# A convolution module's input product: six of sixteen channel blocks take both halves of the activations in one product and add two partial sums

## The chip, the cores and the metric

One core of a Trainium2 chip runs the whole program. The metric is the device time of one execution in microseconds (us); smaller is better. The kernel before was timed three times; the profile is a further execution, recorded by the hardware profiler.

## What is computed

The reference is a small decoder trunk on one sequence of 256 tokens with 2048 channels, all in float32. It has two mixer layers, each followed by a dense MLP, and a last RMSNorm. The change lies in the first mixer, a causal convolution module:

```python
def conv_module(h, w_in, b_in, dw, dw_b, ln_g, ln_b, w_out, b_out):
    u = h @ w_in + b_in                       # (256 x 2048) @ (2048 x 4096)
    a, gate = jnp.split(u, 2, axis=-1)
    v = a * jax.nn.sigmoid(gate)
    v = lax.conv_general_dilated(v, dw[:, None, :], window_strides=(1,),
        padding=[(CONV_WIDTH - 1, 0)], ...)   # 31 taps along the tokens, each channel alone
    v = layer_norm(v + dw_b, ln_g, ln_b)
    return jax.nn.silu(v) @ w_out + b_out

for i in range(DEPTH):                        # DEPTH = 2
    x = x + mixer_i(rms_norm(x, mix_norm[i])) # i = 0: conv_module, i = 1: an S5 layer
    x = x + mlp(rms_norm(x, mlp_norm[i]), w_up[i], w_down[i])
return rms_norm(x, final_norm)
```

## The kernel before

**Products in float32r.** TensorE (PE) multiplies in the type float32r. To keep the accuracy, each float32 operand is split into a high part `hi`, rounded to float32r, and a remainder `lo`. A product is then the sum of three: weight hi by activation hi, weight hi by activation lo, and weight lo by activation hi. Weights stream from memory by the DMA queue of SyncE (`fetch`, L92) into three buffers `raw`; ScalarE (ACT) writes `hi` (L118); VectorE (DVE) or, for most of the input product, GpSimd (POOL) writes `lo` (L125). `hi` and `lo` have four buffers each, and each holds half a weight step. The activations are kept transposed as `hT`: for each of 16 blocks of 128 input channels the 256 tokens of the hi part, and behind them the 256 tokens of the lo part.

**The input product.** `conv_in` makes the product with `w_in` for 16 channel blocks c = 0 to 15, called block 0 to block 15 here. A block is 128 channels of `a` and the 128 of its `gate`: two accumulators (m = 0, 1) in PSUM. `acc2` hands out PSUM tiles of 2 x 512 float32 numbers for each partition; there are two of them, so block c+2 can begin only when the last reader of block c is done. A block has four weight half steps, each with four blocks of input channels (kk). There are two helpers for a half step:

```python
def mm_f(self, accs, xT, hi, lo, k0, first, last):        # used in the MLP's first product
    for kk in range(4):
        for m in range(2):                                # L199: hi by [hi | lo] of x, 512 columns
            mm(accs[m], lhsT=hi[:, kk, cs[m]], rhs=xT(k0 + kk), ...)
    for kk in range(4):
        for m in range(2):                                # L202: lo by hi of x, 256 columns
            mm(accs[m][:, 0:T], lhsT=lo[:, kk, cs[m]], rhs=xT(k0 + kk)[:, 0, :], ...)

def mm_g(self, accs, xT, hi, lo, k0, first, last):        # used in conv_in
            mm(accs[m], lhsT=hi[:, kk, c], rhs=x[:, 0, :], ...)    # L211, 256 columns
            mm(accs[m], lhsT=hi[:, kk, c], rhs=x[:, 1, :], ...)    # L212, 256 columns
            mm(accs[m], lhsT=lo[:, kk, c], rhs=x[:, 0, :], ...)    # L213, 256 columns
```

`mm_g` adds all three products into the same 256 columns of the accumulator. `mm_f` leaves two sums: columns 0 to 255 hold hi by hi and lo by hi, columns 256 to 511 hold hi by the lo half of x, and somebody must add them.

**The gate.** Behind the last half step of block c, `gate(c)` multiplies both accumulators in place by the tokens' RMSNorm factor (DVE, L446, which writes `acc`), takes the sigmoid of the gate half (ACT, L447, tile `ga`), and multiplies (DVE, L448, which reads `acc` and writes the block's channels in `vT`). L448 is the accumulator's last reader.

**The depthwise convolution.** For blocks 0 to 11 `depthwise` starts a PSUM tile `cv` on ACT (L527) and then adds 30 taps on DVE, each one instruction on 128 x 256 numbers (L829); the last of them writes into `vT`. A tap of a channel block needs that block's tap before it. Blocks 12 to 15 are done by PE from shifted copies (tile `pk`, L484).

**The layer norm's early sums.** When the taps of blocks 0 to 3 are done, PE sums their channels into a PSUM tile `stat` (`colsum`, L539, one matmul for each block), and `ln_shift` follows: ACT copies `stat` into a tile `raw` (L558; the weight buffers have the same name, this one has 128 x 256 numbers), PE makes the `mean` of it (L560), DVE scales it to `shift` (L562), DVE subtracts it from the four blocks (`centre`, L569), ACT squares them (L571, tile `sq`), and PE adds both into `stat` (eight matmuls of L539). The copy `raw` is taken from a pool of three buffers, `t2`, from which the tiles `bo` of `add_b_out` (POOL: a DMA of L398 and an addition of L400) and others come too.

**What sets the order.** The program text is traced once. `run_steps` goes through the half steps: it issues loads, splits four half steps ahead, calls `consume` and then the callbacks whose time has come (`after(n, ...)`: n half steps later). A scheduler then writes each engine's instructions into one fixed order, by its own estimate of when each can run, by their place in the program and by the priority that `high_priority` gives them; the gate's instructions and the splits have it (`URGENT`). On the chip every engine runs its list strictly in that order, and waits on semaphores.

Of the kernel before, what the change touches and what calls it, by code (L numbers as in the profile page):

```python
# [12 lines left out]
AF = mybir.ActivationFunctionType  # L13
ALU = mybir.AluOpType
# [4 lines left out]
P = 128  # L19
EPS = 1e-6  # L20
D = 2048
T = 256
# [8 lines left out]
NQ = 4  # L31
EARLY = 4
PACKED = (12, 13, 14, 15)
URGENT = 300


class Trunk:
# [373 lines left out]
    def conv_in(self):  # L411
        w = self.a["conv_w_in"][0].rearrange("(k p) (h c) -> p k h c", p=P, h=2)
        self.fed = set()
        self.tail = []
        self.stat = None
        st = {}
        for c in range(KB):
            for kc in range(2):
                def consume(hi, lo, half, c=c, kc=kc):
                    if kc == 0 and half == 0:  # L420
                        st["acc"] = self.acc2()
                    A = st["acc"][:, :, 0:T]
                    hi, lo = (t.rearrange("p k h c -> p k (h c)") for t in (hi, lo))
                    self.mm_g([A[:, 0], A[:, 1]], self.hT, hi, lo, kc * 8 + half * 4,
                              kc == 0 and half == 0, kc == 1 and half == 1)
# [12 lines left out]
    def cblks(self, c, n):  # L438
        return self.vT2[c // 8][:, c % 8:c % 8 + n, PAD:PAD + T]

    def gate(self, c, A):
        nc = self.nc
        b_in = self.vec("b_in")
        t = self.tmp.tile([P, T], F32, tag="ga", name="ga", bufs=2)
        with self.tc.high_priority(offset=URGENT):
            nc.vector.tensor_tensor(out=A, in0=A, in1=self.rstdB.broadcast_to([P, 2, T]), op=ALU.mult)  # L446
            nc.scalar.activation(t, A[:, 1, :], AF.Sigmoid, bias=b_in[:, KB + c:KB + c + 1])  # L447
            nc.vector.scalar_tensor_tensor(out=self.cblk(c), in0=A[:, 0, :], scalar=b_in[:, c:c + 1], in1=t,  # L448
                                           op0=ALU.add, op1=ALU.mult)
        if c in PACKED:  # L450
            self.depthwise_packed(c)
        else:
            self.depthwise(c)
# [1154 lines left out]
```

## Time and profile before

| what | value |
|---|---|
| time, median of 3 runs | 1988.23 us (1988.21 to 1988.59) |
| the profiled execution's own time | 1987.61 us |
| its span, first to last instruction | 1985.8 us |
| PE busy | 1966.9 us, 99% of the span |
| DVE busy | 1401.3 us, 71% |
| ACT busy | 952.4 us, 48% |
| POOL busy | 274.8 us, 14% |
| input product on PE | about 8 to 214 us of the span |
| DVE busy from 100 to 200 us | 97.2 of 100 us |
| POOL busy from 100 to 150 us | 48.9 of 50 us |

An engine is busy in the profile while one of its instructions runs; matmuls overlap in the pipeline, and their ends are modelled, so their starts are the better measure of pace. A row of the timeline has the start in us from the span's start, the duration, the engine, the line and operation, the tiles (written<-read), the shapes, how many equal ones follow each other (x), and in brackets how long the engine had been idle before, and what ended that. A row for one line of the program gives for its instructions the shortest, median and longest duration in ns and the first and last start. Whatever its share of the whole, an engine matters where another one waits for it.

### The profile page before, as it was taken

The numbers are of one execution on the slowest core, as the hardware profiler recorded it, in microseconds if no ns is written. First come the engines' busy times: TensorE is split into PE (matmuls) and PEld (weight loads), VectorE is DVE, ScalarE is ACT, GpSimd is POOL, SyncE is SP. The second block draws the span as 40 slices with busy tenths as digits, with TensorE's granted clock in tenths as the row PEclk, the third lists the DMA queues.
The fourth block names the chain that finished last, engine by engine and source line by source line (L and its number), as shares of the span: only waits on it lengthen the run. The fifth ranks groups of instructions, "written<-read, shape, count | busy, mean of one in ns | idle before, by whom it ended". The sixth has DMA issues, their size and how long they took to land.

```text
span 1985.8 us, 28885 instructions
## 1 busy us (share of the span) xinstructions
PE 1966.9 (99%) x11604; PEld 1687.0 (85%) x11604; DVE 1401.3 (71%) x1904; ACT 952.4 (48%) x1179; POOL 274.8 (14%) x252
## 2 busy tenths in 40 slices
PE   8999999999999999999999999999999999999998
PEld 8999788888888888888888788888888888888887
DVE  6899798888787777777558847565555565555655
ACT  6443655544444544444445445454444454444444
POOL 3998300000000221222010000000000000000000
PEclk9999999999999999999999999999999999999999
DMA  8767458667686877877898865665666656565653
GB/s 228 190 184 207 147 183 267 206 226 245 200 260 192 214 229 253 265 246 238 319 308 298 304 215 186 191 191 189 193 190 192 190 191 191 190 213 190 192 191 128
DMA packets 317030, 428.49 MB, mean 216 GB/s; under 512 B 9761, under 2 KB 211553, under 8 KB 313537
## 3 DMA queue, kind: packets, MB, share of 16 engines
q1 hardware_dynamic: 300976, 384.59, 61.6%
q0 software_dynamic: 12352, 37.49, 6.3%
q10 hardware_dynamic: 3568, 4.56, 0.8%
q8 instruction: 91, 1.49, 0.3%
q14 instruction: 43, 0.35, 0.1%
HBM read 400.08 MB, written 34.91 MB: 219 GB/s over the span
## 4 chain that ended last, share of the span: by engine, by line
PE 96%; DVE 2%; DMA 1%; issue 0%; SPq 0%; POOL 0%; ACT 0%; POOLq 0%; DVEq 0%; ACTq 0%
PE acc L199 24%; PE acc L222 15%; PE acc L223 15%; PE acc L224 15%; PE acc L202 12%; PE acc L213 3%; PE acc L212 3%; PE acc L211 3%; PE pk L484 1%; DMA Vt<-Vd 0%; SPq L92 0%; PE kp L1113 0%; PE xw L1254 0%; DMA raw<-in_conv_w_in_dram 0%; PE xt L254 0%
## 5 line engine op out<-in xcount | busy, mean ns | idle before, releaser
L118 ACT ACTIVATE hi<-raw 128x1024 fp32r<-128x1024 f32 x672 | 711.6, 1060 | 953.5 <-PE acc L224 510.2
L125 DVE TENSOR_TENSOR lo<-raw,hi 128x1024 fp32r<-128x1024 f32 x611 | 747.9, 1226 | 505.6 <-ACT hi L118 501.3
L199 PE MATMUL acc<-hT,hi 128*128 128x512 f32 x2048 | 514.4, 393 | 0.0
L199 PEld LDWEIGHTS acc<-hT,hi 128*128 128x128 f32 x2048 | 368.9, 189 | 68.0 <-issue 1.6
L222 PE MATMUL acc<-hi,rT 128*128 128x512 f32 x992 | 387.2, 391 | 0.0
L223 PE MATMUL acc<-lo,rT 128*128 128x512 f32 x992 | 386.4, 390 | 0.0
L224 PE MATMUL acc<-hi,rT 128*128 128x512 f32 x992 | 386.0, 389 | 0.0
L202 PEld LDWEIGHTS acc<-hT,lo 128*128 128x128 f32 x2048 | 279.6, 190 | 20.0
L202 PE MATMUL acc<-hT,lo 128*128 128x256 f32 x2048 | 286.3, 282 | 0.0
L222 PEld LDWEIGHTS acc<-hi,rT 128*128 128x128 f32 x992 | 186.3, 188 | 39.6 <-issue 1.6
L224 PEld LDWEIGHTS acc<-hi,rT 128*128 128x128 f32 x992 | 186.3, 188 | 39.1
L223 PEld LDWEIGHTS acc<-lo,rT 128*128 128x128 f32 x992 | 186.3, 188 | 38.0 <-issue 0.2
L125 POOL TENSOR_TENSOR lo<-raw,hi 128x1024 fp32r<-128x1024 f32 x60 | 143.1, 2402 | 31.3 <-ACT hi L118 24.8
L211 PE MATMUL acc<-hT,hi 128*128 128x256 f32 x512 | 146.1, 286 | 0.9 <-ACT hi L118 0.9
L212 PE MATMUL acc<-hT,hi 128*128 128x256 f32 x512 | 145.7, 286 | 0.3 <-DVE hT L259 0.3
L213 PE MATMUL acc<-hT,lo 128*128 128x256 f32 x512 | 145.5, 286 | 0.0
L829 DVE SCALAR_TENSOR_TENSOR cv<-vT,dw,cv 128x256 f32<-128x256 f32 x348 | 141.3, 486 | 2.2 <-ACT cv L527 1.7
L820 DVE TENSOR_TENSOR x<-x,acc 128x1024 f32<-128x1024 f32 (+1 forms) x72 | 83.6, 1161 | 27.6 <-PE acc L224 22.0
L211 PEld LDWEIGHTS acc<-hT,hi 128*128 128x128 f32 x512 | 98.9, 193 | 3.0 <-issue 1.6
L222 PE MATMUL acc<-hi,yT 128*128 128x512 f32 x256 | 101.1, 395 | 0.0
L212 PEld LDWEIGHTS acc<-hT,hi 128*128 128x128 f32 x512 | 98.8, 193 | 2.2 <-issue 1.6
L223 PE MATMUL acc<-lo,yT 128*128 128x512 f32 x256 | 99.9, 390 | 0.6 <-DVE lo L125 0.6
(285 smaller groups left out, 1722.9 us busy)
## 6 DMA issues: line engine op xcount, KB each, us to landing
raw<-in_mlp_w_up_dram SPq DMA_DIRECT2D x128, 1024.0 KB, 5.8
raw<-in_mlp_w_down_dram SPq DMA_DIRECT2D x128, 1024.0 KB, 5.2
raw<-in_ssm_w_glu_dram SPq DMA_DIRECT2D x32, 1024.0 KB, 5.5
raw<-in_conv_w_in_dram SPq DMA_DIRECT2D x60, 512.0 KB, 5.6
raw<-in_conv_w_out_dram SPq DMA_DIRECT2D x16, 1024.0 KB, 5.2
Vd<-bv POOLq DMA_DIRECT2D x16, 512.0 KB, 6.3
Md<-Kd POOLq DMA_DIRECT2D x32, 256.0 KB, 7.2
Wt<-Wd SPq DMA_DIRECT2D x8, 1024.0 KB, 10.1
```

What stands on the lines that cost most here:

```text
L118: self.nc.scalar.activation(hi, sl, AF.Copy)
L125: ins = eng.tensor_tensor(out=lo, in0=sl, in1=hi.bitcast(F32), op=ALU.subtract)
L199: mm(accs[m], lhsT=hi[:, kk, cs[m]], rhs=xT(k0 + kk), start=first and kk == 0, stop=False)
L202: mm(accs[m][:, 0:T], lhsT=lo[:, kk, cs[m]], rhs=xT(k0 + kk)[:, 0, :], start=False, stop=last and kk == 3)
L211: mm(accs[m], lhsT=hi[:, kk, c], rhs=x[:, 0, :], start=first and kk == 0, stop=False)
L212: mm(accs[m], lhsT=hi[:, kk, c], rhs=x[:, 1, :], start=False, stop=False)
L213: mm(accs[m], lhsT=lo[:, kk, c], rhs=x[:, 0, :], start=False, stop=last and kk == 3)
L222: mm(acc[:, b, :], lhsT=ak[:, 0, t], rhs=hi[:, kk, :], start=first and kk == 0, stop=False)
L223: mm(acc[:, b, :], lhsT=ak[:, 0, t], rhs=lo[:, kk, :], start=False, stop=False)
L224: self.mm_last = mm(acc[:, b, :], lhsT=ak[:, 1, t], rhs=hi[:, kk, :], start=False, stop=last and kk == 1)
L820: return self.nc.vector.tensor_tensor(out=out, in0=a, in1=b, op=op)
L829: return self.nc.vector.scalar_tensor_tensor(out=out, in0=a, scalar=s, in1=b, op0=op0, op1=op1)
```

## The change

Blocks 4 to 9 use `mm_f` in place of `mm_g`, and their gate first adds the two halves of the accumulator: ACT copies columns 256 to 511 into a new tile `low` from the pool `t2`, and DVE adds it to columns 0 to 255 in place. The rest of the gate is as it was. Nothing is said about the order of the instructions: the scheduler makes it anew.

```diff
+HALVES = range(4, 10)
...
-                    A = st["acc"][:, :, 0:T]
+                    acc = st["acc"]
+                    A = acc if c in HALVES else acc[:, :, 0:T]
...
-                    self.mm_g([A[:, 0], A[:, 1]], self.hT, hi, lo, kc * 8 + half * 4,
+                    (self.mm_f if c in HALVES else self.mm_g)([A[:, 0], A[:, 1]], self.hT, hi, lo, kc * 8 + half * 4,
...
-                        self.gate(c, A)
+                        self.gate(c, acc)
...
-    def gate(self, c, A):
+    def gate(self, c, acc):
+        A = acc[:, :, 0:T]
...
         with self.tc.high_priority(offset=URGENT):
+            if c in HALVES:
+                low = self.t2([P, 2, T], name="low")
+                nc.scalar.activation(low, acc[:, :, T:2 * T], AF.Copy)
+                self.tt(A, A, low, ALU.add)
             nc.vector.tensor_tensor(out=A, in0=A, in1=self.rstdB.broadcast_to([P, 2, T]), op=ALU.mult)
```

The lists of the engines change between about 65 and 215 us of the old span; ahead of that and behind it they are the same but for numbers in names. The changed file has one line more ahead of `conv_in` and seven more from the gate's L446 on, so that in its rows L199 is L200, L202 is L203, L446 is L453, L447 is L454, L448 is L455, L527 is L534, L539 is L546, L558 is L565, L560 is L567, L562 is L569, L569 is L576, L571 is L578, L820 (a plain DVE operation on two tensors) is L827 and L829 is L836. The new ACT copy is L451. The texts below keep the old numbers, and say where a row has a new one.

Three places are shown. The first is DVE at the gates of blocks 3 and 4, before the change: L446 opens a gate's DVE work and L448 ends it, L829 are the taps.

```order
L446 TENSOR_TENSOR acc<-acc,bcs 128x2x256
L829 SCALAR_TENSOR_TENSOR vT<-vT,dw,cv 128x256
L829 SCALAR_TENSOR_TENSOR cv<-vT,dw,cv 128x256 x2
L448 SCALAR_TENSOR_TENSOR vT<-acc,vecs,ga 128x256
L829 SCALAR_TENSOR_TENSOR cv<-vT,dw,cv 128x256 x22
L446 TENSOR_TENSOR acc<-acc,bcs 128x2x256
L829 SCALAR_TENSOR_TENSOR cv<-vT,dw,cv 128x256 x2
L829 SCALAR_TENSOR_TENSOR vT<-vT,dw,cv 128x256
L829 SCALAR_TENSOR_TENSOR cv<-vT,dw,cv 128x256
L448 SCALAR_TENSOR_TENSOR vT<-acc,vecs,ga 128x256
```

The first gate here is that of block 3, the second that of block 4: 22 taps stand between them. After the change the same place, from the last row of block 3's gate, reads:

```order
L455 SCALAR_TENSOR_TENSOR vT<-acc,vecs,ga 128x256
L836 SCALAR_TENSOR_TENSOR cv<-vT,dw,cv 128x256 x25
L836 SCALAR_TENSOR_TENSOR vT<-vT,dw,cv 128x256
L836 SCALAR_TENSOR_TENSOR cv<-vT,dw,cv 128x256 x26
L836 SCALAR_TENSOR_TENSOR vT<-vT,dw,cv 128x256
L836 SCALAR_TENSOR_TENSOR cv<-vT,dw,cv 128x256 x8
L836 SCALAR_TENSOR_TENSOR vT<-vT,dw,cv 128x256
L827 TENSOR_TENSOR acc<-acc,low 128x2x256
L569 TENSOR_SCALAR shift<-mean 128x256
L453 TENSOR_TENSOR acc<-acc,bcs 128x2x256
L576 TENSOR_TENSOR vT<-vT,shift 128x4x256
L827 TENSOR_TENSOR acc<-acc,low 128x2x256
```

Between the end of block 3's gate and the first DVE work of block 4's stand 62 taps now, all that blocks 1 to 3 still had to do; the last nine of them (x8 and the one that writes `vT`) are of block 3 alone, each needing the one before. Behind block 4's addition come the shift, block 4's L446, the subtraction from four blocks and block 5's addition; only then, in the next row of the list (`L455`, not shown), block 4's L448.

The second place is ACT, where the new copies `low` of blocks 4 and 5 stand in the changed kernel. `raw<-stat` is the copy of the early sums.

```order
L119 ACTIVATE hi<-raw 128x1024 x7
L565 ACTIVATE raw<-stat 128x256
L451 ACTIVATE low<-acc 128x512 x2
L454 ACTIVATE ga<-acc,vecs 128x256
L578 ACTIVATE sq<-vT 128x1024
L534 ACTIVATE cv<-vT,vecs,dw 128x256
L454 ACTIVATE ga<-acc,vecs 128x256
```

Both copies stand behind `raw<-stat`, which before the change came behind the sigmoid of block 6 (`ga`). The copy of the sums needs all taps of blocks 0 to 3.

The third place is PE in the changed kernel, from the end of block 5 (`acc_1071`) into block 6 (`acc_1197`), with the numbers in the names; block 4 is `acc_924`, and `acc_1197` has the same PSUM banks.

```order
L203 MATMUL acc_1071<-hT_109,lo_1068 128x256 x8
L546 MATMUL stat_430<-vT_252,ones_100 32x256 x2
L567 MATMUL mean_943<-raw_941,q4_246 128x256
L546 MATMUL stat_430<-vT_252,ones_100 32x256 x4
L200 MATMUL acc_1197<-hT_108,hi_1088 128x512 x8
L203 MATMUL acc_1197<-hT_108,lo_1089 128x256 x8
L200 MATMUL acc_1197<-hT_108,hi_1111 128x512 x2
L546 MATMUL stat_430<-sq_948,ones_100 32x256 x4
```

The sums of blocks 2 and 3, the mean and the first four later sums stand between block 5 and block 6 now; before, they stood inside the products of blocks 6 and 7. The first matmul of block 6 waits for block 4's L448, as in every pair of blocks.

More of the change, by code (lines that the diff above doesn't have):

```diff
@@ L421, in consume @@
                         st["acc"] = self.acc2()
-                    A = st["acc"][:, :, 0:T]
+                    acc = st["acc"]
+                    A = acc if c in HALVES else acc[:, :, 0:T]
                     hi, lo = (t.rearrange("p k h c -> p k (h c)") for t in (hi, lo))
-                    self.mm_g([A[:, 0], A[:, 1]], self.hT, hi, lo, kc * 8 + half * 4,
-                              kc == 0 and half == 0, kc == 1 and half == 1)
+                    (self.mm_f if c in HALVES else self.mm_g)([A[:, 0], A[:, 1]], self.hT, hi, lo, kc * 8 + half * 4,
+                                                              kc == 0 and half == 0, kc == 1 and half == 1)
                     if kc == 1 and half == 1:
-                        self.gate(c, A)
+                        self.gate(c, acc)
                 if c >= 2:
```

## The prediction

> **What bounds the kernel now.** The page of the profile comes first: the engines' busy time and the chain of work that ended last.
>
> ```profile
> PE 1966.9 (99%) x11604; PEld 1687.0 (85%) x11604; DVE 1401.3 (71%) x1904; ACT 952.4 (48%) x1179; POOL 274.8 (14%) x252
> PE 96%; DVE 2%; DMA 1%; issue 0%; SPq 0%; POOL 0%; ACT 0%; POOLq 0%; DVEq 0%; ACTq 0%
> ```
>
> PE is the bound: 99% busy, and 96% of the chain. So the question for any edit is how long PE works or stands still; a microsecond of PE standing still in the middle is one at the end, unless PE would have had to wait later anyway. Next comes PE's timeline at the starts of blocks 3, 4 and 6 in the input product.
>
> ```profile
> 50.20 0.28 PE L211 MATMUL acc<-hT,hi 128*128 128x256 f32 x1
> 61.72 0.28 PE L211 MATMUL acc<-hT,hi 128*128 128x256 f32 x1
> 86.23 0.28 PE L211 MATMUL acc<-hT,hi 128*128 128x256 f32 x1
> ```
>
> Block 3 takes 61.72 - 50.20 = 11.52 us for 96 matmuls, which is 0.120 each. Blocks 4 and 5 take 24.51 together: 2 x 11.52, and the rest is sums for the layer norm. PE doesn't wait there. The third view is DVE's timeline, since the change moves DVE's list most.
>
> ```profile
> 64.57 0.48 DVE L448 SCALAR_TENSOR_TENSOR vT<-acc,vecs,ga 128x256 f32<-128x256 f32 x1
> 64.96 8.71 DVE L829 SCALAR_TENSOR_TENSOR cv<-vT,dw,cv 128x256 f32<-128x256 f32 x22
> 74.17 0.70 DVE L446 TENSOR_TENSOR acc<-acc,bcs 128x512 f32<-128x512 f32 x1 [0.51 <-PE acc L213]
> ...
> 86.43 0.70 DVE L446 TENSOR_TENSOR acc<-acc,bcs 128x512 f32<-128x512 f32 x1 [2.15 <-PE acc L213]
> ...
> 88.60 1.66 DVE L829 SCALAR_TENSOR_TENSOR cv<-vT,dw,cv 128x256 f32<-128x256 f32 x4
> 90.17 0.48 DVE L829 SCALAR_TENSOR_TENSOR vT<-vT,dw,cv 128x256 f32<-128x256 f32 x1
> 90.56 4.16 DVE L829 SCALAR_TENSOR_TENSOR cv<-vT,dw,cv 128x256 f32<-128x256 f32 x8
> 94.75 0.48 DVE L829 SCALAR_TENSOR_TENSOR vT<-vT,dw,cv 128x256 f32<-128x256 f32 x1
> 98.68 0.70 DVE L446 TENSOR_TENSOR acc<-acc,bcs 128x512 f32<-128x512 f32 x1 [3.45 <-PE acc L213]
> ```
>
> Here DVE waits for PE: at the gates of blocks 4, 5 and 6 it stood idle for 0.51, 2.15 and 3.45 us until the block's product was done. The gate runs as soon as it can, and the taps fill the time between gates. That keeps the accumulator free well ahead of the block that needs it next.
>
> **The change part by part.** *The product itself* gets cheaper. A half step of `mm_f` can be read in the MLP, where it stands already:
>
> ```profile
> 372.07 2.00 PE L199 MATMUL acc<-hT,hi 128*128 128x512 f32 x8
> 373.91 1.12 PE L202 MATMUL acc<-hT,lo 128*128 128x256 f32 x8
> ...
> 374.86 2.00 PE L199 MATMUL acc<-hT,hi 128*128 128x512 f32 x8
> ```
>
> From one half step to the next are 374.86 - 372.07 = 2.79 us, so a block of four takes 11.16, and 11.52 - 11.16 = 0.36 us are saved in each of six blocks: 2.2 us in all, and no more, since the columns are as many as before and a third of the matmuls goes.
>
> *The two additions* have their prices in the MLP too, on the same shapes (first a copy of half an accumulator by ACT, then its addition by DVE):
>
> ```profile
> L807 ACT ACTIVATE t<-acc x64: 576/586/602, 340.0 to 1890.7; 128x512 f32<-128x512 f32 x64
> L808 DVE TENSOR_TENSOR t<-acc,t x64: 677/684/687, 341.2 to 1892.0; 128x512 f32<-128x512 f32 x64
> ```
>
> Six of each are 3.5 us on ACT and 4.1 us on DVE. By themselves they are hidden: ACT waits most of the time, and DVE's 4.1 us find their cover in its 2 to 3 us of idle time at each of these gates. If that cover were gone, the next accumulator would still have a whole block, 11 us, of room.
>
> *The order* is where the time goes. Block 4's addition on DVE stands behind 62 taps and needs `low`; `low` stands on ACT behind `raw<-stat`; that waits for PE's sum of block 3, hence for the last of the 62 taps. And block 6 waits on PE for block 4's L448. Neither list can be overtaken, so I add up this path from 64.96, where the taps behind block 3's gate begin, and which nothing in the change moves. Taps of two or three channel blocks in turn go at 0.392 us: five of them from 88.60 to 90.56. Taps of one block alone go slower: nine from 90.56 to 94.75 + 0.48 = 95.23, 4.67 us. The 62 are 53 of the first kind and 9 of the second: 64.96 + 53 x 0.392 + 4.67 = 90.4. PE's block 5 is over at 61.72 + 2 x 11.16 + 2 x 0.62 (a sum in each) = 85.3, and PE stands still from there. What follows the last tap has rows in the old run (PE's sums and mean, ACT's copy, DVE's shift and subtraction):
>
> ```profile
> 100.01 0.62 PE L539 MATMUL stat<-vT,ones 128*32 128x256 f32 x2
> 103.41 0.59 PE L560 MATMUL mean<-raw,q 128*128 128x256 f32 x2
> 109.56 0.64 PE L539 MATMUL stat<-vT,ones 128*32 128x256 f32 x8
> 100.67 0.39 ACT L558 ACTIVATE raw<-stat 128x256 f32<-128x256 f32 x1 [0.62 <-PE stat L539]
> 104.04 0.42 DVE L562 TENSOR_SCALAR shift<-mean 128x256 f32<-128x256 f32 x1
> 105.17 1.68 DVE L569 TENSOR_TENSOR vT<-vT,shift 128x1024 f32<-128x1024 f32 x1
> ```
>
> The chain is: sum 0.62, copy `raw` 0.39, copy `low` 0.59, block 4's addition 0.68, shift 0.42, L446 0.70, subtraction 1.68, block 5's addition 0.68, L448 0.48. Together 6.24 us; less some 0.3 for instructions of one engine that overlap a little, and with 0.5 to 1 for the steps from engine to engine (`raw` began 0.04 after the sum's end), 6.6. Block 6 begins at 97.0 in place of 86.23: **10.8 us late**, after PE has stood still for 11.7.
>
> Of this, some comes back. Two sums of 0.62, the mean of 0.59 and four sums of 0.64, 2.5 us, lay between the products of blocks 6 and 7; in the new list they are done within the wait. Blocks 6 to 9 save 4 x 0.36 = 1.4 us; what blocks 4 and 5 save only makes the wait longer.
>
> *The clock* takes some again. The start of the trace shows PE after it stood idle, its matmuls of 256 columns every 0.21 us until 13.2 and every 0.12 from then on; the end shows the granted clock falling after PE's last work (the last two rows: a stretch, its length, the busy time of PE, PEld, DVE, ACT and POOL, the granted clock, and DMA):
>
> ```profile
> 7.95 0.58 PE L211 MATMUL acc<-hT,hi 128*128 128x256 f32 x1 [0.91 <-ACT hi L118]
> ...
> 12.80 0.41 PE L213 MATMUL acc<-hT,lo 128*128 128x256 f32 x1
> 13.02 0.41 PE L211 MATMUL acc<-hT,hi 128*128 128x256 f32 x1
> 13.23 0.33 PE L212 MATMUL acc<-hT,hi 128*128 128x256 f32 x1
> 13.40 0.28 PE L213 MATMUL acc<-hT,lo 128*128 128x256 f32 x1
> 13.52 0.27 PE L254 MATMUL xt<-ident,x 128*128 128x128 f32 x1
> ...
> 1978.20:1982.80 4.60, 0.00 (x0) 0.00 (x0) 2.23 (x7) 1.12 (x2) 0.56 (x1) 1.00 0.96 354
> 1982.90:1985.80 2.90, 0.00 (x0) 0.00 (x0) 0.00 (x0) 0.00 (x0) 0.00 (x0) 0.50 0.39 146
> ```
>
> Without PE work (0.00, x0) the clock stayed at 1.00 for 4.6 us and was then 0.50. A wait of 11.7 us is longer, with only a handful of small matmuls in it. Work at half pace loses 1 - 0.12/0.21 = 0.43 of its time. How long it lasts is open: nothing, if the small matmuls count as work; at the start it lasted from the first matmul of block 0 at 7.95 to 13.2, 5.3 us, with transposes ahead of it, which would be 2.3 us lost, or 3.5 with an 8 us that takes in work ahead of it. I take 4.6 us, nearer to the start's, so **2.0 us** lost. The Trainium skill, "TensorE: Matmul & The Clock Gate", Part 1, says that an idle window of about 3.4 us halves PE's clock and a busy one of about 3.4 us restores it. By that, an estimate, the loss would be 1.5 us and the sum 8.4 in place of 8.9. The trace agrees with the halving; its start took longer than 3.4 us to recover.
>
> *The sum:* 10.8 - 2.5 - 1.4 + 2.0 = +8.9 us. The profiled execution, 1987.61 with its span of 1985.8, would be 1996.5; it lies 0.6 under the median of 1988.23, so the median becomes **1997.1 us**, 0.45% slower. Behind block 6 DVE is no new bound: its next gate has 32 taps ahead of it, 12.5 us, and the accumulator it frees is wanted a block after that. At the end of the input product DVE was waiting for PE before:
>
> ```profile
> 214.49 0.70 DVE L446 TENSOR_TENSOR acc<-acc,bcs 128x512 f32<-128x512 f32 x1 [1.73 <-PE acc L213]
> ```
>
> So a later PE there makes all that follows later by as much.
>
> **The rivals.** *The clock isn't halved:* the small matmuls in the wait keep it up. For it: the fall came after 4.6 us without any PE work, and there is some here, near the end of the wait. Against it: from 85.3 to 90.4 are 5 us with next to none. Result 1995.1.
>
> *POOL stops PE a second time.* It has one `lo` and more for each half step:
>
> ```profile
> L125 POOL TENSOR_TENSOR lo<-raw,hi 128x1024 fp32r<-128x1024 f32 x60 | 143.1, 2402 | 31.3 <-ACT hi L118 24.8 <-DVE rowsel L896 6.4
> L400 POOL TENSOR_TENSOR x<-x,bo 128x1024 f32<-128x1024 f32 x4 | 9.6, 2391 | 0.0
> L386 POOL TENSOR_TENSOR wpk<-dp,m 128x1024 f32<-128x1024 f32 x4 | 7.7, 1920 | 0.0
> L398 POOL DMA_DIRECT2D bo<-in_conv_b_out_dram x4: 566/580/624, 102.1 to 123.3; - x4
> ```
>
> Four `lo` are 9.6 us, and over blocks 7 to 11 come three additions of 2.39, two masks of 1.92 and three DMA issues of 0.58, 12.8 us or 2.6 for each block. So POOL needs 12.2 for a block, against 11.2 to 11.5 on PE: short by 4 us over five blocks. Against it: a `lo` is begun most of a block ahead, some 5 us, and POOL does one addition within the wait. If it decides, it costs up to 3 us: 2000.1.
>
> *No wait at all,* the one on the other side: if block 4's gate came on DVE before block 5 is over on PE, only the saving of 6 x 0.36 = 2.2 us would be left, 1986.0, which is no measurable change. It would need the 62 taps and the chain behind them in 20 us, and the taps alone took 25 at the pace of the old run. Only a pace near 0.2 us per tap would decide for it, and no row shows one.
>
> **How the numbers follow.** About 0.2%, 4 us, is what a measurement of this kernel can tell from no change. The forecast has a chance of 0.72, the clock that stays 0.12, POOL's stop 0.09, no wait 0.07. The open terms are the clock (0 to 3.5) and the hand-overs (a microsecond either way), so the forecast itself reaches from 1994 to 2000; with the first two rivals the range is 1993.5 to 2000.5, and it leaves out the third. Faster by over 0.2% has 0.02, within 0.2% 0.06 (1984.3 to 1992.2), slower 0.92.
>
> **What would show it.** Right: in the profile of the changed kernel, PE idle for 10 to 13 us before the first matmul of block 6, ended by DVE or by the sums' chain; DVE busy with taps meanwhile; then matmuls at about 0.43 us per 512 columns for a few microseconds; blocks 7 to 9 at 11.2 us; no other new wait on PE; and the end of block 15 some 9 us later than 214.4. Wrong: block 6 begins before 90, or PE's wait is there and the total doesn't show it, because a later wait shrinks by as much; or PE stops again behind POOL.

## The result, and the profile after

The changed kernel takes 2004.41 us (median of 5 runs, 2002.99 to 2005.47), the kernel before on the same chip 1988.23 (1987.42 to 1989.26). The ratio is 1.008, with a 95% interval of 1.0066 to 1.0093: 16.2 us slower, where 8.9 were forecast. The direction was right; the size was not, and lies outside the range of 1993.5 to 2000.5.

The page of the changed kernel, engine PE and the chain of waits:

```profile
PE 1970.5 (98%) x11412; PEld 1678.5 (84%) x11412; DVE 1410.9 (70%) x1910; ACT 955.9 (48%) x1185; POOL 275.9 (14%) x252
PE 85%; DVE 1%; DMA 0%; issue 0%; ACT 0%; POOL 0%; SPq 0%; POOLq 0%; DVEq 0%
```

PE does about as much as before (1970.5 us for 1966.9), in a span of 2002.6 us in place of 1985.8, and it has less of the chain (85% for 96%). So it stands still for longer, and its timeline says where:

```profile
85.35 0.62 PE L546 MATMUL stat<-vT,ones 128*32 128x256 f32 x2
89.94 0.62 PE L546 MATMUL stat<-vT,ones 128*32 128x256 f32 x2 [3.97 <-DVE vT L836]
91.03 1.22 PE L567 MATMUL mean<-raw,q 128*128 128x256 f32 x2 [0.47 <-ACT raw L565]
94.50 1.08 PE L546 MATMUL stat<-vT,ones 128*32 128x256 f32 x8 [2.25 <-DVE vT L576]
95.58 3.75 PE L200 MATMUL acc<-hT,hi 128*128 128x512 f32 x8
...
174.68 1.08 PE L546 MATMUL stat<-vT,ones 128*32 128x256 f32 x8 [5.15 <-DVE vT L576]
```

The first wait is the one forecast: block 5's product is over at 85.35, the chain of sums follows, and block 6 begins at 95.58. The second wait was not forecast. It lies in the middle of block 12, where PE's list now has the sums of blocks 4 to 7, and lasts 5.15 us until DVE has written `vT` by the subtraction (L569 before, L576 now). Before, these sums stood in block 14. The windows of both kernels, cut at the starts of block 4, of block 6, of block 12 (twice: before and behind it) and at the end of block 15, give the sum (of the changed kernel first, then of the one before; columns as in the prediction's two window rows):

```profile
61.22:95.58 34.36, 27.55 (x148) 20.72 (x147) 32.38 (x77) 13.52 (x17) 26.98 (x13) 0.93 0.72 191
95.58:110.06 14.48, 14.48 (x73) 11.98 (x74) 14.07 (x35) 5.38 (x7) 9.54 (x5) 0.82 0.08 23
110.06:166.62 56.56, 56.56 (x387) 52.54 (x386) 52.79 (x129) 26.45 (x33) 55.22 (x28) 1.00 0.71 193
166.62:186.90 20.28, 15.13 (x115) 13.09 (x114) 20.28 (x35) 6.61 (x8) 13.31 (x6) 0.83 0.43 115
186.90:230.88 43.98, 43.98 (x442) 39.80 (x444) 32.24 (x71) 15.73 (x19) 30.10 (x13) 1.00 0.77 215
```

```profile
61.72:86.23 24.51, 24.51 (x199) 23.42 (x197) 22.05 (x55) 9.78 (x11) 21.47 (x10) 1.00 0.65 177
86.23:98.48 12.25, 12.25 (x100) 11.71 (x99) 8.53 (x19) 4.61 (x5) 11.40 (x6) 1.00 0.64 173
98.48:159.15 60.67, 60.63 (x502) 58.66 (x501) 58.18 (x142) 27.51 (x33) 59.08 (x30) 1.00 0.65 176
159.15:170.67 11.52, 11.52 (x98) 11.52 (x97) 11.52 (x30) 4.72 (x5) 11.52 (x5) 1.00 0.88 240
170.67:214.45 43.78, 43.78 (x438) 39.06 (x440) 40.91 (x94) 17.45 (x22) 31.10 (x14) 1.00 0.80 223
```

| stretch | forecast | measured |
|---|---|---|
| blocks 4 and 5, and the wait | +10.8 | 34.36 - 24.51 = +9.85 |
| blocks 6 to 11 | -2.5 - 1.4 + 2.0 = -1.9 | 71.04 - 72.92 = -1.9 |
| block 12 | 0 | 20.28 - 11.52 = +8.8 |
| blocks 13 to 15 | 0 | 43.98 - 43.78 = +0.2 |

Block 4 itself began 0.5 us earlier, and behind block 15 another 0.4 us are lost; with these the stretches make up the 16.8 us between the two spans. Up to the start of block 12 the forecast holds within a microsecond; as much again is lost in block 12, and that is what there is to explain. What DVE and POOL did there (DVE first):

```profile
166.71 0.88 DVE L836 SCALAR_TENSOR_TENSOR cv<-vT,dw,cv 128x256 f32<-128x256 f32 x2
167.50 7.13 DVE L576 TENSOR_TENSOR vT<-vT,shift 128x1024 f32<-128x1024 f32 x1
```

```profile
161.81 2.40 POOL L401 TENSOR_TENSOR x<-x,bo 128x1024 f32<-128x1024 f32 x1
164.19 9.35 POOL L126 TENSOR_TENSOR lo<-raw,hi 128x1024 fp32r<-128x1024 f32 x4
177.94 2.37 POOL L126 TENSOR_TENSOR lo<-raw,hi 128x1024 fp32r<-128x1024 f32 x1 [4.40 <-ACT hi L119]
```

The subtraction shows no wait in brackets, yet it takes 7.13 us, where the same instruction took 1.22 at 93.23, with POOL idle. It ends at 174.63, which is 1.09 after POOL's row of four `lo` has ended (164.19 + 9.35 = 173.54). The rows for the line say that this was no single case, before the change (first) and after it:

```profile
L569 DVE TENSOR_TENSOR vT<-vT,shift x3: 1683/1737/2411, 105.2 to 210.6; 128x1024 f32<-128x1024 f32 x3
```

```profile
L576 DVE TENSOR_TENSOR vT<-vT,shift x3: 1216/3439/7128, 93.2 to 217.9; 128x1024 f32<-128x1024 f32 x3
```

In all five cases with POOL at work the end lies 1.08 to 1.09 us behind the end of a POOL instruction. So the 1.68 us that the prediction took as the instruction's price was 0.6 us of standing still and 1.09 of work. The theory to test: **this subtraction, which reads both inputs from SBUF (where every tile of the kernel lies that isn't in PSUM), isn't let in while POOL works without a pause.** The rival: DVE is simply late at that place, whatever it does there and whatever POOL does.

### The profile page after: what moved, and what is told of

The parts are those of the page before. It is cut to its first block, busy times and chain, and to the rows that moved or that the text cites. A ratio compares the mean times of both kernels' runs of the same rounds, so it can differ in the third digit from the quotient of the medians.

```text
span 2002.6 us, 28518 instructions
## 1 busy us (share of the span) xinstructions
PE 1970.5 (98%) x11412; PEld 1678.5 (84%) x11412; DVE 1410.9 (70%) x1910; ACT 955.9 (48%) x1185; POOL 275.9 (14%) x252
## 4 chain that ended last, share of the span: by engine, by line
PE 85%; DVE 1%; DMA 0%; issue 0%; ACT 0%; POOL 0%; SPq 0%; POOLq 0%; DVEq 0%
PE acc L200 24%; PE acc L223 15%; PE acc L224 15%; PE acc L225 15%; PE acc L203 12%; DMA Vt<-Vd 0%; PE kp L1120 0%; PE xw L1261 0%; PE xt L255 0%; PE acc L234 0%; PE acc L233 0%; PE acc L235 0%; PE mv L1353 0%; DVE S L827 0%; DVE lo L126 0%
## 5 line engine op out<-in xcount | busy, mean ns | idle before, releaser
L200 PE MATMUL acc<-hT,hi 128*128 128x512 f32 x2240 | 565.1, 394 | 0.0
L200 PEld LDWEIGHTS acc<-hT,hi 128*128 128x128 f32 x2240 | 404.3, 189 | 76.3 <-issue 3.5
L203 PEld LDWEIGHTS acc<-hT,lo 128*128 128x128 f32 x2240 | 306.6, 191 | 22.0
L203 PE MATMUL acc<-hT,lo 128*128 128x256 f32 x2240 | 313.9, 283 | 0.0
L836 DVE SCALAR_TENSOR_TENSOR cv<-vT,dw,cv 128x256 f32<-128x256 f32 x348 | 142.2, 485 | 2.2 <-ACT cv L534 1.5
L827 DVE TENSOR_TENSOR x<-x,acc 128x1024 f32<-128x1024 f32 (+1 forms) x72 | 83.6, 1161 | 27.7 <-PE acc L225 22.0
L223 PE MATMUL acc<-hi,yT 128*128 128x512 f32 x256 | 101.1, 395 | 0.0
L225 PE MATMUL acc<-hi,yT 128*128 128x512 f32 x256 | 99.7, 390 | 0.0
L212 PE MATMUL acc<-hT,hi 128*128 128x256 f32 x320 | 92.0, 288 | 0.9 <-ACT hi L119 0.9
L213 PE MATMUL acc<-hT,hi 128*128 128x256 f32 x320 | 91.5, 287 | 0.3 <-DVE hT L260 0.3
L214 PE MATMUL acc<-hT,lo 128*128 128x256 f32 x320 | 91.7, 288 | 0.0
```

The source lines that it names most:

```text
L200: mm(accs[m], lhsT=hi[:, kk, cs[m]], rhs=xT(k0 + kk), start=first and kk == 0, stop=False)
L212: mm(accs[m], lhsT=hi[:, kk, c], rhs=x[:, 0, :], start=first and kk == 0, stop=False)
L213: mm(accs[m], lhsT=hi[:, kk, c], rhs=x[:, 1, :], start=False, stop=False)
L214: mm(accs[m], lhsT=lo[:, kk, c], rhs=x[:, 0, :], start=False, stop=last and kk == 3)
L223: mm(acc[:, b, :], lhsT=ak[:, 0, t], rhs=hi[:, kk, :], start=first and kk == 0, stop=False)
L225: self.mm_last = mm(acc[:, b, :], lhsT=ak[:, 1, t], rhs=hi[:, kk, :], start=False, stop=last and kk == 1)
```

## The experiments

Every diff is against the changed kernel unless said otherwise. The kernel before ran beside each and took 1987.5 to 1988.0 us.

**1. `low` in a buffer of its own.**

```diff
-                low = self.t2([P, 2, T], name="low")
+                low = self.tmp.tile([P, 2, T], F32, tag="low", name="low", bufs=1)
```

> The changed kernel, with the copy `low` in a buffer of its own instead of one of the three that it shares with the layer norm's copy `raw`. Theory (the shared buffers tie block 4's gate to the sums of blocks 0 to 3): the gate of block 4 comes before the chain of sums, PE does not stand still ahead of block 6, the sums of blocks 4 to 7 stand in block 14 again, and what is left is the cheaper product, 6 x 0.36 = 2.2 us: 1986 us against the kernel before (1988.2), ratio about 0.999. Rival (the two added instructions or the one-product form themselves cost the time): PE still stands still for some microseconds in blocks 6 to 12 and the time stays above 1995.

Measured: 1999.0 us, ratio 1.0055 (1.0041 to 1.0068). The order is as expected: block 6 follows block 5 without a wait, the sums of blocks 4 to 7 stand in block 14. So the first wait is the order that the shared buffers force. But the time is 13 us above the theory's 1986; it lies where the rival had it, and PE does stand still in block 8. It waits there for the first subtraction, that of blocks 0 to 3, and once more, 2.95 us at 228.34, behind block 15 for DVE. PE, DVE and POOL in block 8:

```profile
120.16 1.08 PE L546 MATMUL stat<-vT,ones 128*32 128x256 f32 x8 [7.70 <-DVE vT L576]
```

```profile
107.44 12.66 DVE L576 TENSOR_TENSOR vT<-vT,shift 128x1024 f32<-128x1024 f32 x1
```

```profile
107.18 2.41 POOL L401 TENSOR_TENSOR x<-x,bo 128x1024 f32<-128x1024 f32 x1
109.54 4.70 POOL L126 TENSOR_TENSOR lo<-raw,hi 128x1024 fp32r<-128x1024 f32 x2
114.20 1.90 POOL L387 TENSOR_TENSOR wpk<-dp,m 128x1024 f32<-128x1024 f32 x1
116.05 0.59 POOL L399 DMA_DIRECT2D bo<-in_conv_b_out_dram  x1
116.66 2.35 POOL L401 TENSOR_TENSOR x<-x,bo 128x1024 f32<-128x1024 f32 x1
122.71 2.37 POOL L126 TENSOR_TENSOR lo<-raw,hi 128x1024 fp32r<-128x1024 f32 x1 [3.69 <-ACT hi L119]
```

The subtraction came 0.26 us behind the start of an unbroken row on POOL, and ends at 120.10, 1.09 after the row does (119.01). In the old run it came at 105.17, about 2 us earlier, and was through by 106.85.

**2 and 3. The subtraction with one input in PSUM, and its control.** In both, blocks 4 to 11 are centred one by one, by as many instructions; they stand one tap apart, and the input lies in PSUM in one and in SBUF in the other.

```diff
 # one input in PSUM: in depthwise(), ahead of the last tap
+            if j == TAPS - 1 and c >= EARLY:
+                self.tt(acc, acc, self.shift, ALU.subtract)
 # control: in depthwise(), behind the last tap
+        if c >= EARLY:
+            self.tt(self.cblk(c), self.cblk(c), self.shift, ALU.subtract)
 # both, in centre()
-        nc.vector.tensor_tensor(out=v, in0=v, in1=self.shift..., op=ALU.subtract)
+        if c < EARLY:
+            nc.vector.tensor_tensor(out=v, in0=v, in1=self.shift..., op=ALU.subtract)
```

> The changed kernel, with the layer norm's subtraction of blocks 4 to 11 done block by block on the accumulator in PSUM ahead of the last tap, so that it has one input in SBUF and not two; the sums of blocks 4 to 7 stay in PE's list inside block 12. Theory (a DVE instruction with both inputs in SBUF isn't let in while POOL works without a pause): no subtraction takes over 0.6 us, PE's wait of 5.15 us in block 12 and the halved clock behind it (about 2.3) go, the wait of block 6 stays: 2004.4 - 7.4 = 1997 us. Rival (DVE is simply behind at that place, whatever the operand): PE still waits 4 to 5 us in block 12 and the time stays between 2002 and 2006.

> The control of the run with the subtraction in PSUM: as many subtractions, block by block at the same place, but behind the last tap on the convolution's result, so with both inputs in SBUF. Theory (POOL keeps such instructions out): some of these subtractions take 2 to 7 us in place of 0.5, above all those of blocks 4 to 7 between 140 and 175 us, and the time is 2000 to 2008. Rival (the operand makes no difference): each takes 0.4 to 0.6 us and the time is that of the PSUM form within 1 us.

Measured: 2000.64 us (ratio 1.0063, 1.0051 to 1.0076) with PSUM, 2006.77 (1.0094, 1.0080 to 1.0108) in SBUF. The eight subtractions with one input in PSUM (first row) and those of the control (second), with shortest, median and longest in ns:

```profile
L830 DVE TENSOR_TENSOR cv<-cv,shift x8: 423/428/432, 126.2 to 214.7; 128x256 f32<-128x256 f32 x8
```

```profile
L830 DVE TENSOR_TENSOR vT<-vT,shift x8: 412/418/6984, 126.8 to 221.2; 128x256 f32<-128x256 f32 x8
```

The long one of the control and POOL beside it:

```profile
158.76 6.98 DVE L830 TENSOR_TENSOR vT<-vT,shift 128x256 f32<-128x256 f32 x1
```

```profile
158.49 2.38 POOL L401 TENSOR_TENSOR x<-x,bo 128x1024 f32<-128x1024 f32 x1
160.84 4.62 POOL L126 TENSOR_TENSOR lo<-raw,hi 128x1024 fp32r<-128x1024 f32 x2
168.51 2.40 POOL L126 TENSOR_TENSOR lo<-raw,hi 128x1024 fp32r<-128x1024 f32 x1 [3.05 <-ACT hi L119]
```

It ends at 165.74, 0.28 behind POOL's 165.46, and PE waits 4.87 us for it in block 11. The operand makes 6.1 us of difference, and the rival falls. The Trainium skill, "SBUF — State Buffer", section "Who interferes with whom", says that a DVE instruction with two SBUF inputs contends with a GpSimd instruction that reads SBUF, that one with at most one SBUF input doesn't, outside the modes in which DVE uses two ports for one input, and that whichever issues first holds the port for its whole instruction while the other fully blocks. The trace agrees on who contends. It differs on how long: in the long stalls DVE did not get in when the running POOL instruction ended, but only when POOL paused, past five of its instructions in the first experiment.

The theory is too strong, though: POOL's first pause let DVE in at the latest, but a pause was not always needed. Another subtraction of the control (DVE first, then POOL):

```profile
126.76 2.52 DVE L830 TENSOR_TENSOR vT<-vT,shift 128x256 f32<-128x256 f32 x1
```

```profile
126.59 7.62 POOL L126 TENSOR_TENSOR lo<-raw,hi 128x1024 fp32r<-128x1024 f32 x3
```

It ends at 129.28, 0.28 behind the first of these three `lo`, and POOL's row runs on without a pause. The row lets in a second subtraction at 131.56, for 0.41 us, and takes 7.62 in all, where three `lo` in a row took 7.13 in experiment 2. The subtraction of blocks 8 to 11 in experiment 11 got in the same way. What decides who comes first between two POOL instructions, no run here shows.

The PSUM form missed its 1997 by 3.6 us. PE's sums of single blocks no longer stand in groups of four, and that accounts for it: a block with one such sum takes 12.25 us in place of 11.52; in blocks 9 to 15 this is 3 to 4 us. Experiment 6 prices it by itself.

**4. PE's sums later.** The eight sums of blocks 4 to 7 come as a callback 20 half steps later.

```diff
-        self.colsum(self.stat[:, 0, :], cs, ...)
-        self.colsum(self.stat[:, 1, :], cs, ...)
+        def sums():
+            self.colsum(self.stat[:, 0, :], cs, ...)
+            self.colsum(self.stat[:, 1, :], cs, ...)
+        if c == 4:
+            self.after(20, sums)
+        else:
+            sums()
```

> The changed kernel, with PE's eight sums of blocks 4 to 7 put off by 20 half steps, so that they stand at the end of block 15 in PE's list; the subtraction stays where it is. Theory (the stall of DVE costs only because PE's sums stand right behind it): the subtraction still takes 3 to 8 us, but PE does not wait in block 12, nothing else becomes late, and the time is 2004.4 - 7.4 = 1997 us. Rival (DVE's lost 6 us come back as a later wait of PE for a gate): PE waits 3 us or more in blocks 13 to 15 and the time is above 2000.

Measured: 2000.65 us, ratio 1.0064 (1.0051 to 1.0076). The subtraction took 6.97 us, ending 1.09 behind POOL's row again. Here the rival is nearer: without the sums PE still waited 2.70 us in block 12, now for the gate's last instruction (L455), which stands behind the stalled subtraction in DVE's list, and the block took 15.86 us. So the stall costs in two ways, and the place of the sums is 2004.41 - 2000.65 = 3.8 us of it, about half of the 7.4 expected.

**5. Both causes taken away.** The buffer of its own; the PSUM form for blocks 4 to 11; and for blocks 0 to 3 a subtraction that reads the mean in PSUM, in place of the one in `centre`:

```diff
+        v = self.cblks(0, EARLY)
+        self.stt(v, ps.unsqueeze(1).broadcast_to([P, EARLY, T]), -1.0 / (EARLY * P), v, ALU.mult, ALU.add)
```

> The changed kernel with both causes taken away at once: the copy `low` in a buffer of its own, and all of the layer norm's subtractions with one input in PSUM (those of blocks 0 to 3 read the mean there, those of blocks 4 to 11 the accumulator). Theory (the time of the change is the shared buffers and the subtraction that POOL keeps out, nothing else): no wait of PE over 1 us in blocks 4 to 13, and what is left is the cheaper product, 1988.2 - 2.2 = 1986 us, at most 2 more for DVE's few more instructions at the end of the convolution. Rival (DVE's added work, 4.1 us for the additions, is itself a bound): PE waits 2 us or more for DVE in block 14, in block 15 or behind it, and the time is 1990 or more.

Measured: 1991.84 us, ratio 1.0022 (1.0013 to 1.0031). PE has no wait over 0.3 us in blocks 4 to 13: both waits are explained. But the 2.2 us of the cheaper product don't show; PE waits 1.89 and 0.42 us for DVE at 221.28 and 222.32, behind block 15. The rival took this one.

**6. The control for it:** the product of the kernel before with the same subtractions. Against experiment 5:

```diff
-HALVES = range(4, 10)
+HALVES = range(0, 0)
```

> The product of the kernel before (no block takes the one product), with all subtractions of the layer norm with one input in PSUM. Theory (before, the subtraction's stalls of 0.5 to 1.3 us hit nobody): 1988 us within 2. Rival (the other form of the subtraction is itself worth something): below 1985 or above 1991.

Measured: 1991.16 us, ratio 1.0017 (1.0008 to 1.0025), 3.2 us slower, with no new wait on PE. Blocks 10 and 11 took 12.99 and 12.25 us in place of 11.52 and 11.65, for the single sums. The rival took this one: the form has a price by itself. Taken off experiment 2 it gives 2000.64 - 3.2 = 1997.4, the time expected there. From experiment 5 it can't be taken off in the same way: experiment 9, where the sums of blocks 4 to 11 are back in their groups, took as long as experiment 5.

**7. The gate's two instructions without the product.** `mm_g` everywhere, but the copy and a DVE instruction in the gates of blocks 4 to 9.

```diff
-                    A = acc if c in HALVES else acc[:, :, 0:T]
+                    A = acc[:, :, 0:T]
...
-                    (self.mm_f if c in HALVES else self.mm_g)(...)
+                    self.mm_g(...)
...
+                acc = acc[:, :, 0:T]
                 low = self.t2([P, 2, T], name="low")
-                nc.scalar.activation(low, acc[:, :, T:2 * T], AF.Copy)
-                self.tt(A, A, low, ALU.add)
+                nc.scalar.activation(low, acc, AF.Copy)
+                self.tt(A, A, low, ALU.max)
```

> The changed kernel with the old product of three matmuls in all blocks, but with the two added instructions in the gates of blocks 4 to 9 on the same shapes and buffers (a copy `low` of half the accumulator, and a maximum of the two in place of the addition, which leaves the values as they were). Theory (the waits come from where the gate's instructions stand, not from the product): PE stands still ahead of block 6 and again in block 12 for the sums, and the time is that of the changed kernel and the 2.2 us that the product no longer saves: 2004 to 2008 us. Rival (the one-product form shifts the lists by itself): one of the two waits is gone and the time is below 2000.

Measured: 2005.93 us, ratio 1.0088 (1.0074 to 1.0102), with 3.52, 0.47 and 2.25 us ahead of block 6 and 5.05 us in block 12. Both waits come with the gate's two instructions alone, without the new product. Against the changed kernel's 2004.41 the product would be worth 1.5 us, but single runs of the two overlap (2004.47 to 2006.49 here, 2002.99 to 2005.47 there).

**8. All sixteen blocks** by the one product, otherwise as 5: `HALVES = range(0, 16)`.

> As the run with both causes taken away, with the one product in all sixteen blocks. Theory (PE is the bound once both waits are gone): 1988.2 - 16 x 0.36 = 1982.4 us. Rival (DVE becomes the bound of the convolution's last blocks, with 16 additions of 0.68 us and later sums): PE waits several us for DVE around block 15 and the time is 1986 or more.

Measured: 1999.85 us, ratio 1.0057 (1.0044 to 1.0071). The rival, and by far: PE waits 5.60 and 3.19 us for DVE behind block 15.

**9. Only the first subtraction with one input in PSUM,** and `low` in its own buffer, so that the sums keep their groups.

```diff
+        v = self.cblks(0, EARLY)
+        self.stt(v, ps.unsqueeze(1).broadcast_to([P, EARLY, T]), -1.0 / (EARLY * P), v, ALU.mult, ALU.add)
...
-        nc.vector.tensor_tensor(out=v, in0=v, in1=self.shift..., op=ALU.subtract)
+        if c >= EARLY:
+            nc.vector.tensor_tensor(out=v, in0=v, in1=self.shift..., op=ALU.subtract)
```

> The run with `low` in a buffer of its own, and of the subtractions only the first (blocks 0 to 3) with one input in PSUM; the other two as they were, so that PE's sums keep their groups of four. Theory (in the run with `low` alone, 12.66 us of that subtraction were POOL's): it takes 1.2 to 1.8 us, PE's wait of 7.7 in block 8 and some 1.9 of halved clock go: 1999.0 - 9.6 = 1989.4, and at most 3 less if PE's later wait of 2.95 us for DVE goes too: 1986 to 1990. Rival (DVE can't keep the pace with or without POOL): PE waits elsewhere in blocks 8 to 14 and the time stays above 1994.

Measured: 1991.76 us, ratio 1.0021 (1.0011 to 1.0030). The stall of 12.66 us and PE's wait of 7.70 are gone, and 7.2 us with them. The end is 1.8 above the theory's band: PE now waits 4.09 us behind block 15, for DVE's copies `R` (the shifted copies for the packed blocks), where experiment 1 waited 2.95 us, and DVE has next to no idle time ahead of them (PE first; then a window of DVE with its busy time, the granted clock and DMA):

```profile
220.62 1.46 PE L491 MATMUL pk<-R,wpk 128*32 128x256 f32 x9 [4.09 <-DVE R L477]
```

```profile
206.00:218.00 12.00, 11.99 (x31) 1.00 0.29 92
```

**10. The same from POOL's side:** `low` in its own buffer, subtractions as they were, POOL's additions late.

```diff
-            self.after(20 + 8 * i, lambda i=i: self.add_b_out(i))
+            self.after(60 + 2 * i, lambda i=i: self.add_b_out(i))
```

> The run with `low` in a buffer of its own, subtractions unchanged (both inputs in SBUF), but POOL's four additions to x with their DMA issues put off to the end of the input product, so that POOL has pauses earlier. Theory (the subtraction gets in when POOL pauses): that of blocks 0 to 3 takes at most 3.7 us (one instruction of POOL's, and itself) in place of 12.66, PE waits at most 2 us for it, and the time is 1986 to 1991. Rival (something other than POOL holds it): it takes over 7 us and the time stays near 1999.

Measured: 1996.78 us, ratio 1.0050 (1.0037 to 1.0062). The subtraction of blocks 0 to 3 took 3.06 us, and PE did not wait in blocks 4 to 14: the mechanism as expected. The time missed, because PE waits 5.69 us and more behind block 15.

**11. POOL's additions late in the changed kernel,** by the same two lines, and nothing else.

> The changed kernel, where only POOL's four additions to x and their DMA issues are put off to the end of the input product; buffers, gates and subtractions as in the changed kernel. Theory (the second wait is POOL's unbroken row of work): the subtraction of blocks 4 to 7 takes at most 3.7 us in place of 7.13, PE waits at most 1 us in block 12, the wait of block 6 stays: 2004.4 - 7.4 = 1997 us, and up to 3 more where POOL's additions now fall at the end. Rival (POOL isn't the cause): the subtraction still takes over 5 us and the time stays above 2001.

Measured: 2007.11 us, ratio 1.0095 (1.0080 to 1.0110). The time is above the rival's 2001, yet up to the end of block 15 the theory is right: block 15 ends at 223.46 in place of 230.88, 7.4 us earlier. POOL's row now has pauses of 0.46 to 0.49 us, and one is enough (DVE first):

```profile
169.28 1.61 DVE L576 TENSOR_TENSOR vT<-vT,shift 128x1024 f32<-128x1024 f32 x1
```

```profile
167.41 2.40 POOL L126 TENSOR_TENSOR lo<-raw,hi 128x1024 fp32r<-128x1024 f32 x1 [0.49 <-ACT hi L119]
170.27 2.89 POOL L126 TENSOR_TENSOR lo<-raw,hi 128x1024 fp32r<-128x1024 f32 x1 [0.47 <-ACT hi L119]
```

The subtraction ends at 170.89, 1.08 behind POOL's 169.81, and POOL's next `lo` takes 2.89 in place of 2.40: it waits in its turn. PE has no wait in block 12. The gain is lost at the end, where POOL's additions now meet the eight copies `R` (DVE, then POOL):

```profile
225.41 11.83 DVE L477 COPY R<-vT 32x284 f32<-32x284 f32 x8
```

```profile
226.67 2.36 POOL L126 TENSOR_TENSOR lo<-raw,hi 128x1024 fp32r<-128x1024 f32 x1
...
231.16 4.64 POOL L401 TENSOR_TENSOR x<-x,bo 128x1024 f32<-128x1024 f32 x2
```

In the kernel before they took 3.89 us together. PE waits 9.16 us for them. Two of the eight took nearly all of it: one of 3.43 us ends at 229.20, 0.17 behind that `lo`, and one of 6.32 at 235.97, 0.17 behind the second addition; the others took 0.30 to 0.42. In the kernel before, the first copy took 1.69 and ended 0.16 behind a `lo` (217.94), the seven behind it 0.30 each. That POOL held these copies too, though they have one input each, is argued from these rows and wasn't tried by itself. Both long ones began during DMA issues of POOL, whose part in it stays open, and so does whether the copies ran in one of the two-port modes that the sentence on one input leaves out.

**12. The one product without the additions.** As 9, with the copy and the addition left out.

```diff
-            if c in HALVES:
-                low = ...
-                nc.scalar.activation(low, acc[:, :, T:2 * T], AF.Copy)
-                self.tt(A, A, low, ALU.add)
```

> The one product in blocks 4 to 9 without the two added instructions of the gate, so the second halves' sums are left out of the result; the first subtraction with one input in PSUM. Theory (the product alone is worth 6 x 0.36 = 2.2 us, and the additions cost DVE's time only at the end of the convolution): 1988.2 - 2.2 = 1986 us, and 0 to 3 below the same kernel with the additions (the run with `low` in its own buffer and the first subtraction in PSUM). Rival (DVE's work doesn't count): the same time as that run within 0.5 us.

Measured: 1985.86 us, ratio 0.9993 (0.9984 to 1.0002), 1.6 us below the kernel before, with an interval that includes no change, and 5.9 below experiment 9, more than the 0 to 3 expected. So the product is worth some 1.6 us at best, not clear of noise, and the two added instructions cost it all and more.

**13 and 14. The one product in blocks 0 to 5, and 2 to 5,** otherwise as 9: `HALVES = range(0, 6)` and `range(2, 6)`.

> As the run with `low` in a buffer of its own and the first subtraction with one input in PSUM, but the one product in blocks 0 to 5, where DVE had idle time, and not in blocks 4 to 9. Theory (the additions cost only where DVE is full, which it is from block 8 on): PE saves up to 6 x 0.36 = 2.2 us and DVE is no later than before: 1986 to 1988.5. Rival (the additions make DVE late wherever they stand): 1990 to 1993, as the same kernel with blocks 4 to 9.

> The same with blocks 2 to 5 alone, so that the first two blocks, which wait for data, are as before. Theory: 4 x 0.36 = 1.4 us saved: 1986.5 to 1988.5. Rival (additions cost wherever they stand): 1989.5 to 1992.

Measured: 1991.43 us (ratio 1.0017, 1.0009 to 1.0026) and 1990.4 (1.0010, 1.0001 to 1.0019). The theory, that early additions are free, falls. DVE's instructions of the taps' line up to 160 us show why. Of the kernel before, of 12, of 9 and of 14, one after the other (the stretch, its length, their busy time and in brackets their number, the granted clock, and DMA; in the last three one of them is the subtraction of blocks 0 to 3, which has the same line there):

```profile
0.00:160.00 160.00, 102.04 (x252) 1.00 0.73 197
```

```profile
0.00:160.00 160.00, 102.99 (x253) 1.00 0.74 200
```

```profile
0.00:160.00 160.00, 99.41 (x242) 1.00 0.74 199
```

```profile
0.00:160.00 160.00, 100.11 (x244) 1.00 0.75 199
```

By 160 us, 252 taps are done without the additions, 241 and 243 with them: 9 to 11 taps, about 4 us at 0.392 each, are pushed behind that point, early additions or late ones (in 9, three of the eleven were missing at 61 us already, ahead of its first addition). From 110 us on DVE is full, and what is late there stays late. Ahead of 110 it had idle time, but the additions didn't go into it. DVE's busy time of the kernel before, of 9 and of 14:

```profile
61.00:110.00 49.00, 40.93 (x97) 1.00 0.68 184
```

```profile
61.00:110.00 49.00, 41.20 (x97) 1.00 0.70 190
```

```profile
61.00:110.00 49.00, 39.36 (x94) 1.00 0.68 184
```

DVE stood idle for about as long with the additions as without, so they took the place of taps. Why the lists leave it so stays open. Most of the 5.9 us between 9 and 12 is spent behind block 15. The profiled executions are 5.8 apart in span; block 15 ends at 212.93 and 211.83, so 1.1 is lost ahead of that and 4.7 behind it. There PE waits 4.09 in place of 0.76 for the copies `R`, and the granted clock is 0.50 at 220.3 to 223.6 and at 230.6 to 233.9, while it stays at 1.00 there in 12.

No version here beats the kernel before by what can be measured: even without the additions it is 1.6 us, within the noise.

## Why the prediction was right in direction and wrong in size

- **"Behind block 6 DVE is no new bound": this step failed.** It looked at the next gate and its accumulator only. The sums of blocks 4 to 7 stand in PE's new list in block 12 in place of 14, right behind a subtraction for which the prediction had no term, and that one stood still for 6 us behind POOL. That is 8.8 us in block 12, where the prediction had none: the wait of 5.15, about 2.3 for a second stretch of halved clock (4.62 of PE's work at 0.50), and the sums themselves, which moved there. DVE was not full in the changed kernel ahead of this place (52.79 of 56.56 us busy); it was held up there. Experiments 2, 4 and 11 take this wait away or shorten it, each by another of its conditions.
- **The price of the subtraction, 1.68 us, was mis-sized, both ways.** It was 1.09 to 1.22 of work and the rest standing still behind POOL. In the first wait, with POOL idle, it took 1.22, which is 0.5 of the 1.4 us by which block 6 began earlier than forecast (95.58, not 97.0); another 0.5 is block 4's earlier start, and the rest the steps between the engines. In block 12 it took 7.13.
- **The first wait** is right in place, cause and, within a microsecond, size: the chain through the shared buffers, 9.9 us for 10.8, and gone as soon as `low` has its own buffer. Experiment 2, which leaves this wait and takes the second one away, would be 1997.4 without the 3.2 us of its form, near the forecast's 1997.1; that sum is argued, no run is that kernel. Of the prediction's signs of being right, "no other new wait on PE" failed, and with it the end of block 15, which came 230.88 - 214.45 = 16.4 us later in place of some 9.
- **The clock** fell as forecast:

```profile
90.70:100.80 10.10, 7.51 (x26) 5.17 (x27) 9.12 (x19) 5.50 (x9) 2.99 (x2) 0.50 0.38 97
172.60:179.30 6.70, 4.62 (x27) 2.78 (x27) 6.70 (x13) 2.48 (x3) 2.30 (x2) 0.50 0.82 218
```

  Blocks 6 to 11 cost in sum what the terms said, -1.9 us, with 2.0 for the clock. It was restored about 5.3 us after block 6 began, 100.9 against 95.58, as at the start, where the prediction took 4.6; by its own working that is 2.3 us. So the rival in which the clock stays up fell. The wait of 5.15 us was long enough for a second stretch.
- **The saving of the product,** 2.2 us, came out as 1.5 and 1.6 in experiments 7 and 12, neither clear of noise. "By themselves they are hidden", said of the additions, is wrong: with both waits gone they cost 5.9 us (experiment 9 against 12).
- **The rivals.** "POOL stops PE a second time" came nearest: POOL did have no time left in blocks 7 to 11, and PE did stop a second time. But not for a `lo`: PE waited for DVE, which POOL kept out. "No wait at all" fell with the first wait.

## What to carry to other kernels

Before an instruction's duration is taken as its price, compare several of its kind with what the neighbour engine does at that moment: a duration that ends a fixed time behind another engine's instruction is a wait that the profile doesn't bracket. Where one engine's list moves by a few microseconds, look for every place at which another engine runs without a pause, and at what stands right behind it in all lists, not only in the next gate. And an engine that is full for a hundred microseconds is a bound there, though it is busy for 70% of the span: that it waits at some gates doesn't make added work free.

## What the runs showed of the hardware

- DVE's `tensor_tensor` with both inputs in SBUF stood still through whole rows of POOL instructions, for up to 12.66 us with its own 1.09, and was let in at POOL's first pause at the latest; a pause of 0.47 us was enough, and POOL then lost 0.49 itself. A DMA issue of 0.59 us between two POOL instructions was no such pause in experiment 1. Three times, in experiments 3 and 11, it got in between two POOL instructions that followed each other without a pause. With one input in PSUM, the subtraction of one block took 0.42 to 0.43 us all eight times; with both in SBUF 0.41 to 6.98.
- Eight copies from SBUF to SBUF took 11.83 us beside POOL's work in experiment 11, 3.89 in the kernel before; the long ones end 0.16 to 0.17 us behind a POOL instruction.
- Eight sums of single blocks in place of two groups of four cost PE about 3.2 us (experiment 6).
